# Candidate rows turned on TensorE instead of sent through DRAM, later column sums, and a new order in the last blocks and the first expert

## The chip, the cores and the metric

The kernel runs on one core of one Trainium2 chip. The metric is the time of one execution on the device, in microseconds (us). The engines are named as in the profile: PE is TensorE, DVE is VectorE, ACT is ScalarE, POOL is GpSimd, and SP is SyncE, which here only issues DMAs.

## The reference

One layer works on x of 2048 tokens by 1024 features (float32). `m` holds six modulation vectors made from the conditioning vector c.

```
h   = modulate(rms_norm(x), sh1, sc1)
b, c_, v = split(h @ w_in)                        # 1024 x 3072
x   = x + g1 * ((b * conv3(c_ * v)) @ w_out)      # short gated convolution
h2  = modulate(rms_norm(x), sh2, sc2)
aff = softmax(h2 @ w_router)                      # 16 experts
g, idx = top_k(aff.T, 256)                        # each expert picks its 256 best tokens
for each expert e:
    xs  = h2[idx[e]]
    hid = silu(xs @ w_gate[e]) * (xs @ w_up[e])
    x[idx[e]] += g2 * (g[e] * (hid @ w_down[e]))
```

So before an expert can work, the 256 greatest of 2048 values of its column of aff must be known, in which order does not matter beyond the pairing of g and idx.

## The kernel before, in words

A float32 product is done as three products of halves: high x high, low x high and high x low. The high half of a weight piece is a rounding copy by ACT (L247, tile `raw` to tile `ws`), the low half is what is left, a subtraction by DVE (L257). A piece is 128 by 2 by 512 elements, 512 KB. `raw` has five buffers in the expert stage. `split_high(n)` and `split_low(n)` emit the splits of all pieces up to n, and `split_to(n)` both.

The order of instructions on each engine is written out by hand: an engine works through its instructions in the order of the program's text, and only semaphores between engines delay it.

The stages, in this order: modulation, input product and convolution (to some 530 us); the output product by 16 blocks of 128 tokens, tb = 0 to 15; the choice of tokens; the experts.

The output product of a block takes eight steps k = 0 to 7 of TensorE (`out_mm`, L1196 to L1199, from pieces of the convolved input that DVE splits at L1094). Behind each step, `behind(tb, k)` emits some of the work on the block before: residual sum (`out_res`, DVE L1211, L1213, L1202), mean square (ACT L1214), norm (`out_h2`, DVE L1289, whose row goes to DRAM by POOL), the two 16-bit planes of the row (`halves_out`, ACT L1260), which SP stores and loads back transposed by a transposing DMA (L1265), joins (`router_join`, DVE L1274, ACT L1275 and L1277, DVE L1282), and the router's products (L1322, L1323, L1361), softmax (`router_sm`, to `aff` at DVE L1381). Blocks from 10 on are transposed by PE instead (`turn_xt`, `direct_mm`). SP also loads x's block (L1187) and the next convolved block (L1087).

For expert 0 the choice is made as the blocks go by. A candidate c is the column of 128 values of aff that block c gives. The values of the candidates so far are held as rows in the tile `ranked`, the same on all partitions. `rank_a(c)` compares all held values with candidate c's own (DVE L1439, with a count) and finds equal ones (POOL L1442, L1443). `rank_b(c)` sums the comparison's columns on PE into the PSUM tile `pr` (L1449), and `rank_c(c)` subtracts these sums from the counts (DVE L1454). `sort_a` to `sort_d` turn counts into a sorted list of 256 (one-hot comparisons L1460, products on PE, a copy on ACT, sums on POOL); this happens for candidates 0 to 7, then with 8 to 11, then with 12 to 14. A candidate's value column becomes a row in one of two ways. `row_store(c)` sends it to the DRAM tensor `values` by SP (L1416, 128 elements of 4 bytes), and `row_load(c)` reads it back to all partitions (L1421). `row_turn` transposes it on PE (L1428) and copies it with ACT (L1429). The table `steps`, made by `plan()`, says at which (block, step) each of these is emitted; the third number orders those of one step. Two PSUM buffers (pool `tp`) serve all of these small products.

After the last block follows a chain: the last sort, the gathers of expert 0's tokens (`fetch_first`, POOL), the router for block 15 (`last_row`, `router_sm`), the correction of the list by block 15's values, and the transposes of the gathered rows.

The experts come next. `gate_up(e, h)` makes half h of gate and up in eight steps (L1870, 24 products of 256 columns a step), and `down(e, dh)` a half of the down product in four (L1947 to L1949). Inside the steps, `between(k)` emits the choice for the other experts. For experts 1 and 2 it is `search_few`: in each round five thresholds are compared, some on DVE (L347), some on ACT (L351), the counts spread (DVE L354), summed on PE (L361, tile `pc`) and judged on DVE (L363 and on). For the other 13 it is `search_all`: a round has one threshold on DVE (L1690), two on ACT (L1694), a sum on PE (L1700) and the judgement on DVE (L1702 to L1708); `tick` emits one round. Gathering, transposing and joining of the next expert's tokens are `pick`, `turn` and `join`.

## Time and profile before

| | us |
|---|---|
| median of three runs | 1893.42 |
| the three runs | 1892.06, 1893.42, 1896.95 |
| the profiled execution | 1892.12 |
| its span, first to last instruction | 1890.3 |
| PE busy | 1815.3 |
| DVE busy | 1293.9 |
| ACT busy | 915.9 |
| POOL busy | 351.6 |

The mean granted clock of PE over the span was 0.983. Stages by the trace: blocks 6 to 10 of the residual work from 601 to 697 us, the last chain to 785.7, expert 0's gate and up to 841.3, expert 1's to 931.6. A table of windows gives, for each stretch, its length and then each engine's busy time with the count of its instructions, PE's granted clock, the share of the DMA engines and GB/s. A row of waits reads: engine, line that waited, what released it, us in total, times, the longest.

### The profile page before, as it was taken

The numbers are of one execution on the slowest core, as the hardware profiler recorded it, in microseconds if no ns is written. First come the engines' busy times: TensorE is split into PE (matmuls) and PEld (weight loads), VectorE is DVE, ScalarE is ACT, GpSimd is POOL, SyncE is SP. The second block draws the span as 40 slices with busy tenths as digits, with TensorE's granted clock in tenths as the row PEclk, the third lists the DMA queues.
The fourth block names the chain that finished last, engine by engine and source line by source line (L and its number), as shares of the span: only waits on it lengthen the run. The fifth ranks groups of instructions, "written<-read, shape, count | busy, mean of one in ns | idle before, by whom it ended". The sixth has DMA issues, their size and how long they took to land.

```text
span 1890.3 us, 29839 instructions
## 1 busy us (share of the span) xinstructions
PE 1815.3 (96%) x11542; PEld 1613.5 (85%) x11542; DVE 1293.9 (68%) x1924; ACT 915.9 (48%) x1263; POOL 351.6 (19%) x546
## 2 busy tenths in 40 slices
PE   7999999999999788897999999999999999999997
PEld 6888888888887666786999999999999999999996
DVE  6787778889766655686756666765666576566653
ACT  5565455334444443455544553544455355445542
POOL 2424101121012434301002102110210221021002
PEclk9999999999999889898999999999999999999999
DMA  9746665655689984566787879788887978888774
GB/s 340 239 168 205 197 211 178 157 160 174 162 262 235 183 155 153 167 202 167 217 239 246 227 224 264 219 245 243 253 228 224 260 223 242 246 250 230 224 229 83
DMA packets 316782, 403.25 MB, mean 213 GB/s; under 512 B 109652, under 2 KB 181248, under 8 KB 316640
## 3 DMA queue, kind: packets, MB, share of 16 engines
q1 hardware_dynamic: 291024, 310.08, 55.3%
q0 software_dynamic: 25616, 91.26, 17.5%
q8 instruction: 90, 1.47, 0.3%
q14 instruction: 52, 0.43, 0.1%
HBM read 316.86 MB, written 63.46 MB: 201 GB/s over the span
## 4 chain that ended last, share of the span: by engine, by line
PE 55%; DVE 4%; ACT 1%; issue 1%; POOL 1%; DMA 1%; POOLq 0%; ACTq 0%; DVEq 0%
PE pm L1870 36%; PE pm L1947 6%; PE pm L1949 6%; PE pm L1948 6%; DVE ws L257 1%; DMA ranked<-values 1%; ACT hit L1694 0%; DVE xt L1213 0%; DVE hit L347 0%; DVE u L1211 0%; PE pi L1803 0%; ACT ws L247 0%; DVE u L1202 0%; PE pm L1196 0%; DMA xs<-hscr,idx 0%
## 5 line engine op out<-in xcount | busy, mean ns | idle before, releaser
L1870 PE MATMUL pm<-xT,ws 128*128 128x256 f32 x6144 | 712.6, 278 | 0.5 <-DVE ws L257 0.5
L1870 PEld LDWEIGHTS pm<-xT,ws 128*128 128x128 f32 x6144 | 709.4, 189 | 3.2 <-DVE ws L257 0.9
L257 DVE TENSOR_TENSOR ws<-raw,ws 128x1024 fp32r<-128x1024 f32 x389 | 462.7, 1222 | 272.7 <-ACT ws L247 272.2
L247 ACT ACTIVATE ws<-raw 128x1024 fp32r<-128x1024 f32 x389 | 393.2, 1051 | 395.3 <-PE pm L1870 314.3
L1977 POOL DMA_INDIRECT out_dram<-ot,idx x30 | 100.6, 3354 | 600.0 <-DVE ot L1966 596.0
L1947 PE MATMUL pm<-ws,hT 128*128 128x512 f32 x504 | 201.1, 399 | 0.0
L1949 PE MATMUL pm<-ws,hT 128*128 128x512 f32 x504 | 200.4, 398 | 0.0
L1948 PE MATMUL pm<-ws,hT 128*128 128x512 f32 x504 | 199.2, 395 | 0.0
L899 PE MATMUL pm<-tg,sb 128*128 128x512 f32 x472 | 184.8, 391 | 0.8 <-ACT cx L966 0.8
L901 PE MATMUL pm<-tg,sb 128*128 128x512 f32 x472 | 183.8, 389 | 0.0
L900 PE MATMUL pm<-tg,sb 128*128 128x512 f32 x472 | 183.8, 389 | 0.0
L879 DVE TENSOR_TENSOR sb<-raw,sb 128x512 fp32r<-128x512 f32 x144 | 99.0, 690 | 59.3 <-ACT sb L878 58.0
L878 ACT ACTIVATE sb<-raw 128x512 fp32r<-128x512 f32 x144 | 88.7, 626 | 64.6 <-DVE raw L887 14.5
L1949 PEld LDWEIGHTS pm<-ws,hT 128*128 128x128 f32 x504 | 96.0, 191 | 20.6
L1948 PEld LDWEIGHTS pm<-ws,hT 128*128 128x128 f32 x504 | 96.1, 191 | 19.9
L1947 PEld LDWEIGHTS pm<-ws,hT 128*128 128x128 f32 x504 | 95.9, 190 | 19.1
L1196 PE MATMUL pm<-ws,hl 128*128 128x512 f32 x256 | 109.5, 428 | 0.1
L1811 POOL DMA_INDIRECT xs<-hhalf,idx x30 | 42.5, 1416 | 337.6 <-issue 212.8
L899 PEld LDWEIGHTS pm<-tg,sb 128*128 128x128 f32 x472 | 88.6, 188 | 19.5 <-ACT cx L966 1.2
L1197 PE MATMUL pm<-ws,hl 128*128 128x512 f32 x256 | 104.6, 408 | 0.0
L901 PEld LDWEIGHTS pm<-tg,sb 128*128 128x128 f32 x472 | 88.6, 188 | 18.5
L900 PEld LDWEIGHTS pm<-tg,sb 128*128 128x128 f32 x472 | 88.6, 188 | 18.0
(446 smaller groups left out, 2361.4 us busy)
## 6 DMA issues: line engine op xcount, KB each, us to landing
raw<-in_moe_w_gate_dram SPq DMA_DIRECT2D x128, 512.0 KB, 5.0
raw<-in_moe_w_up_dram SPq DMA_DIRECT2D x128, 512.0 KB, 4.1
raw<-in_moe_w_down_dram SPq DMA_DIRECT2D x128, 512.0 KB, 4.7
raw<-in_sc_w_in_dram SPq DMA_DIRECT2D x42, 512.0 KB, 4.6
aw<-in_ada_w_dram POOLq DMA_DIRECT2D x32, 512.0 KB, 5.1
xt<-in_x_dram SPq DMA_DIRECT2D x31, 512.0 KB, 6.6
fu<-fscr SPq DMA_DIRECT2D x23, 512.0 KB, 4.5
hl<-in_ada_w_dram SPq DMA_DIRECT2D x32, 256.0 KB, 6.6
```

What stands on the lines that cost most here:

```text
L247: nc.scalar.activation(t[:, 0], raws[n_high], AF.Copy)
L257: (eng or nc.vector).tensor_sub(t[:, 1, ..., s], raw[..., s], t[:, 0, ..., s].bitcast(F32))
L899: nc.tensor.matmul(o, t[:, 0, j], r[:, 0], start=(first and j == 0), stop=False, skip_group_check=True)
L900: nc.tensor.matmul(o, t[:, 1, j], r[:, 0], start=False, stop=False, skip_group_check=True)
L901: nc.tensor.matmul(o, t[:, 0, j], r[:, 1], start=False, stop=end, skip_group_check=True)
L1196: nc.tensor.matmul(ps[h], vh[:, k], w[:, 0, half(h)], start=(k == 0), stop=False)
L1197: nc.tensor.matmul(ps[h], vh[:, k], w[:, 1, half(h)], start=False, stop=False)
L1870: nc.tensor.matmul(o, w[:, i // 2, j, c0], xT[:, i % 2, k], start=(k == i == 0 and f % 2 == 0), stop=(k == KD - 1 and i == 2), skip_group_ ...
L1947: nc.tensor.matmul(ps[s], h, w[:, 0, j], start=(k == 0), stop=False)
L1948: nc.tensor.matmul(ps[s], h, w[:, 1, j], start=False, stop=False)
L1949: nc.tensor.matmul(ps[s], l, w[:, 0, j], start=False, stop=(k == KD - 1))
L1977: st = nc.gpsimd.indirect_dma_start(out=out_rows, out_offset=bass.IndirectOffsetOnAxis(ap=idx_of[e][:, s:s + 1], axis=0), in_=ots[s], in_o ...
```

## The change

1. `row_store`, `row_load` and the tensor `values` are gone. All candidates' rows are made by `row_turn`, the first four in one call with four transposes. The table `plan()` gives each candidate five places: the turn t, the comparison a, the sums b, the count d.
2. `rank_b` is three steps behind `rank_a` for candidates 0 to 7, four for 8, two for 9 to 12, and `rank_c` up to two steps behind `rank_b`. `sort_a` to `sort_d` for candidates 0 to 7 and 8 to 11 move accordingly.
3. In block 15 the norm of block 14, the two last comparisons, their sums and the last sort come at other steps. The two gathers of expert 0 are issued before `best` is summed (`sort_v`), the second one first. The planes of blocks 14 and 15 are copied by POOL instead of ACT.
4. In `search_few` two thresholds are on DVE and three on ACT (before: three and two), and the next base is computed by POOL. It begins one step later. In expert 0's products a piece's low half is split at the step that needs it, and high halves three pieces ahead; its terms are emitted in another order. In `down` the high half is split before the round instead of after it, for expert 0 one piece ahead. `search_all` is spread wider: five of the eight steps of expert 0's down product have a `tick` (before: all), eleven of expert 1's sixteen, and the rest is in expert 2's first products.

The diff, cut to its core:

```diff
-SPLITS = {0: (1, 3, 4, 5, 6, 7, 8, 9), 1: (11, 12, 13, 15, 16, 17, 19, 20)}
+SPLITS = {(0, 0): (0, 1, 2, 3, 4, 5, 6, 7), (0, 1): (9, 10, 11, 12, 13, 14, 15, 16), (1, 0): (28, 29, 30, 31, 32, 33, 34, 35),
+          (1, 1): (37, 38, 39, 40, 41, 43, 44, 45)}
+DOWN_SPLITS = {(0, 0): (18, 19, 20, 21), (0, 1): (23, 24, 25, 26)}
...
-                for j in (3, 4, 0, 1, 2):
+                for j in (2, 3, 4, 0, 1):
                     hit = scratch(j, n)
-                    if j < 3:
+                    if j < 2:
...
-                    nbase = small_tile("nbase", n=2)
-                    nc.vector.tensor_scalar(nbase, biasq[:, it + 1], neg, None, op0=ALU.add)
+                    nbase = small_tile("nbase", n=3)
+                    nc.gpsimd.tensor_scalar(nbase, biasq[:, it + 1], neg, None, op0=ALU.add)
...
-        def halves_out(tb, u, hs=slice(0, 2)):
+        def halves_out(tb, u, hs=slice(0, 2), eng=None):
...
-            nc.scalar.activation(uh[:, hs], u.bitcast(U16).rearrange("p (d h) -> p h d", h=2)[:, hs], AF.Copy)
+            planes = u.bitcast(U16).rearrange("p (d h) -> p h d", h=2)[:, hs]
+            if eng:
+                eng.tensor_copy(uh[:, hs], planes)
+            else:
+                nc.scalar.activation(uh[:, hs], planes, AF.Copy)
...
-        def row_store(c, n=1):
-            nc.sync.dma_start(bass.AP(tensor=values.tensor, offset=values.offset + c * P, ap=[[1, P], [P, n]]),
-                              value(c, n))
-
-        def row_load(c, n=1):
-            i = place(c)
-            nc.sync.dma_start(ranked[:, i * P:(i + n) * P],
-                              bass.AP(tensor=values.tensor, offset=values.offset + c * P, ap=[[0, P], [1, n * P]]))
...
-        def sort_c():
+        def sort_c(values=True):
             pk = small.tile([P, 2, 5], F32, name="pk", tag="pk", bufs=2)
             nc.scalar.activation(pk, pi_of[0], AF.Copy)
+            if values:
+                sort_v(pk)
+            return pk
+
+        def sort_v(pk):
             nc.gpsimd.tensor_add(best, pk[:, :, 2], pk[:, :, 3])
             nc.gpsimd.tensor_add(best, best, pk[:, :, 4])
-            return pk
         def sort_d(pk):
...
         def plan():
-            for c, b, k in ((4, 6, 5), (5, 7, 5), (6, 8, 5), (8, 10, 5), (10, 11, 1)):
-                steps[b, k, 8] = lambda c=c: row_store(c)
-                steps[b + (k == 5), 0 if k == 5 else 4, 8] = lambda c=c: row_load(c)
-            steps[5, 6, 8] = lambda: row_store(0, 4)
-            steps[6, 1, 8] = lambda: row_load(0, 4)
-            for c, a, b in ((0, (6, 4), (6, 7)), (1, (6, 7), (7, 3)), (2, (7, 4), (7, 7)), (3, (7, 7), (8, 3)),
-                            (4, (8, 4), (8, 7)), (5, (8, 7), (9, 3)), (6, (9, 4), (9, 7)), (7, (9, 7), (10, 3)),
-                            (8, (11, 4), (11, 6)), (9, (11, 7), (12, 2)), (10, (11, 7), (12, 3)),
-                            (11, (12, 5), (12, 7)), (12, (13, 6), (14, 1))):
-                steps[(*a, 4 + c % 2)] = lambda c=c: rank_a(c)
-                steps[(*b, 0)] = lambda c=c: rank_b(c)
-                steps[(*((b[0], 3) if c in (9, 10) else b), 1 + c % 2)] = lambda c=c: rank_c(c)
-            steps[9, 7, 3] = lambda: row_turn(7, value(7))
-            steps[11, 7, 3] = lambda: row_turn(3, value(9))
-            steps[12, 4, 3] = lambda: row_turn(5, value(11))
-            steps[13, 5, 4] = lambda: row_turn(2, value(12))
-            pk = []
-            for c, a, b, d in ((7, (10, 4), (10, 7), (11, 1)), (11, (12, 7), (13, 2), (13, 5))):
-                steps[(*a, 6)] = lambda c=c: sort_a(c)
+            for c, t, a, b, d in ((0, (5, 7), (6, 4), (6, 7), (7, 1)), (1, None, (6, 7), (7, 3), (7, 4)),
+                                  (2, None, (7, 4), (7, 7), (8, 1)), (3, None, (7, 7), (8, 3), (8, 4)),
+                                  (4, (6, 7), (8, 4), (8, 7), (9, 1)), (5, (7, 7), (8, 7), (9, 3), (9, 4)),
+                                  (6, (8, 7), (9, 4), (9, 7), (10, 1)), (7, (9, 7), (10, 4), (10, 7), (10, 7)),
+                                  (8, (10, 7), (11, 6), (12, 2), (12, 3)), (9, (11, 7), (12, 4), (12, 6), (12, 7)),
+                                  (10, (11, 5), (12, 5), (12, 7), (12, 7)), (11, (12, 5), (12, 6), (13, 0), (13, 0)),
+                                  (12, (13, 6), (13, 7), (14, 1), (14, 1))):
+                early = -4 if c == 11 else 0
+                if t:
+                    steps[(*t, 7)] = lambda c=c: row_turn(place(c), value(c, 1 if c else 4))
+                steps[(*a, 5)] = lambda c=c: rank_a(c)
+                steps[(*b, early + c % 2)] = lambda c=c: rank_b(c)
+                steps[(*d, early + 2 + c % 2)] = lambda c=c: rank_c(c)
+            for c, a, b, d in ((7, (10, 7), (11, 3), (11, 5)), (11, (13, 0), (13, 2), (13, 4))):
+                steps[(*a, -0.5 if c == 11 else 4)] = lambda c=c: sort_a(c)
                 steps[(*b, 6)] = lambda c=c: (sort_b(c), sort_d(sort_c()))
-                steps[(*d, 3)] = lambda: row_turn(0, best)
+                steps[(*d, 6)] = lambda: row_turn(0, best)
         plan()
         def behind(tb, k):
-            behind_block(tb, k)
-            for t in sorted(t for t in steps if t[:2] == (tb, k)):
-                steps.pop(t)()
+            for early in (True, False):
+                for t in sorted(t for t in steps if t[:2] == (tb, k) and (t[2] < 0) == early):
+                    steps.pop(t)()
+                if early:
+                    behind_block(tb, k)
...
                 router_sm(tb - 1, lambda: out_res(tb, 0, 0))
-                router_gate(tb - 1)
+                out_h2(tb - 1)
                 row_turn(3, value(tb - 2))
                 rank_a(tb - 2)
-                out_res(tb, 0, 1)
-                nc.vector.tensor_scalar(ss_of[tb][:, 2:3], ss_of[tb][:, 0:1], D * EPS, None, op0=ALU.add)
-            if k == 3:
+            if k == 2:
                 row_turn(4, value(tb - 1))
                 rank_a(tb - 1)
+                out_res(tb, 0, 1)
+                router_gate(tb - 1)
+                nc.vector.tensor_scalar(ss_of[tb][:, 2:3], ss_of[tb][:, 0:1], D * EPS, None, op0=ALU.add)
             if k == 4:
-                turn_xt(tb, 0)
                 rank_b(tb - 2)
                 rank_c(tb - 2)
-                out_h2(tb - 1)
                 split_high(first)
-            if k == 6:
+            if k == 5:
                 rank_b(tb - 1)
                 rank_c(tb - 1)
                 sort_a(tb - 1)
+            if k == 6:
+                turn_xt(tb, 0)
             if k == 7:
+                sort_b(tb - 1)
                 direct_mm(tb, 0)
-        sort_b(tb - 1)
-        pk_c = sort_c()
+        pk_c = sort_c(False)
...
+        fetch_first(1)
         fetch_first(0)
+        sort_v(pk_c)
         out_res_last(tb)
         out_rms(tb)
-        fetch_first(1)
         split_high(first + 1)
         out_scale(tb, 1)
         direct_mm(tb, 1)
         xt, u, r = xt_of[tb], u_of[tb], r_of_last[0]
         nc.sync.dma_start(out[0, L - P:L, :], xt)
+        halves_out(tb - 1, u_last[0], eng=nc.gpsimd)
...
-        halves_out(tb - 1, u_last[0])
...
-        nc.scalar.activation(uh[:, :, 0:QT], halves[:, :, 0:QT], AF.Copy)
-        nc.gpsimd.tensor_copy(uh[:, :, QT:D], halves[:, :, QT:D])
+        nc.gpsimd.tensor_copy(uh, halves)
...
-        late = 4 if (e, fh) == (0, 0) else 0
+        low = SPLITS.get((e, fh))
         for k in range(KD):
-            n = SPLITS[fh][k] + w_moe[0, 0, 0, 0] if e == 0 else w_moe[0, e, fh, k // 2] + n_split - 2 + k % 2
-            split_high(n)
+            n = w_moe[0, 0, 0, 0] + low[k] if low else w_moe[0, e, fh, k // 2] + n_split - 2 + k % 2
+            split_high(n + 3 * (e == 0))
             between(k)
             while n_done <= min(n, len(pieces) - 1):
                 split_low(n_done)
-            if k >= late:
+            if e:
                 products(k, (0, 1, 2))
-            elif k % 2:
+            elif (fh, k) == (0, 1):
                 for i in range(3):
+                    for kj in range(2):
+                        products(kj, (i,))
+            elif fh or k:
+                products(k, (0, 1))
+                if k % 2:
                     for kj in (k - 1, k):
-                        products(kj, (i,))
+                        products(kj, (2,))
...
+            low = DOWN_SPLITS.get((e, dh))
+            n = w_moe[0, 0, 0, 0] + low[kk] if low else w_moe[2, e, dh, kk] + n_split - 1
+            split_high(n + 1 if low else n)
             between(kk)
-            split_to(w_moe[2, e, dh, kk] + n_split - 1)
+            split_to(n)
...
-        if (k < 5 if h else k > 0):
+        if (k < 6 if h else k > 1):
             next(first_rounds, None)
-        if (h, k) == (1, 4):
+        if (h, k) == (1, 6):
             pick_oh(1)
-        if (h, k) == (1, 6):
+
+    def first_down(h, kk):
+        if (h, kk) == (0, 0):
             pick(1)
-        if (h, k) == (1, 7):
-            tick(k)
-
-    def first_down(h, kk):
-        tick(kk)
-        if h == 0 and kk < 2:
-            turn(1, kk)
-        if (h, kk) in ((0, 3), (1, 1)):
-            join(1, h)
+        elif (h, kk) not in ((1, 0), (1, 2)):
+            tick(kk)
+        if h == 0 and kk in (1, 2):
+            turn(1, kk - 1)
+        if (h, kk) in ((1, 0), (1, 2)):
+            join(1, kk // 2)
     def second_steps(h, k):
-        if h == 0 or k < 3:
+        if k in ((0, 2, 4, 6, 7), (0, 1, 2, 3, 5, 7))[h]:
             tick(k)
...
+    def third_steps(k):
+        if k < 4:
+            tick(k)
+        if k == 5:
+            for _ in rounds:
+                pass
+            pick_oh(3)
...
-            for _ in rounds:
-                pass
             continue
         else:
-            if e + 1 < E:
+            if 2 < e < E - 1:
                 pick_oh(e + 1)
-            gate_up(e, 0)
+            gate_up(e, 0, third_steps if e == 2 else lambda k: None)
```

Three places where instructions move. The first is SP's queue in blocks 7 and 8; rows are those that SP issues in order, and the DMA of `values` and `ranked` are the candidates' rows. Before:

```order
L1265 DMA_TRANSPOSE hl<-hl 128x16x128
L1087 DMA hl<-vscr 128x8x128
L1187 DMA xt<-in_x_dram 128x1024
L1421 DMA ranked<-values 128x128
L1416 DMA values<-aff 128x1
L1262 DMA hhalf<-hl 128x2048
```

After (line numbers shift with the diff: L1265 is now L1270, L1087 is L1088, L1187 is L1188, L1262 is L1267):

```order
L1270 DMA_TRANSPOSE hl<-hl 128x16x128
L1088 DMA hl<-vscr 128x8x128
L1188 DMA xt<-in_x_dram 128x1024
L1267 DMA hhalf<-hl 128x2048
L1270 DMA_TRANSPOSE hl<-hl 128x16x128
```

Nothing stands between the load of x and the next store of planes any more; twelve DMAs are gone from SP over the blocks.

The second is DVE in block 15, at the last two comparisons (L1439, now L1435), their counts (L1454, now L1450) and the norm of block 14 (L1289, now L1294). Before:

```order
L1439 SCALAR_TENSOR_TENSOR hits,count<-ranked,zero_1695,aff 128x512
L1213 TENSOR_TENSOR xt<-u,xt 128x512
L1202 TENSOR_TENSOR u<-xt,A2b 128x512
L1583 TENSOR_SCALAR ss<-ss 128x1
L1439 SCALAR_TENSOR_TENSOR hits,count<-ranked,zero_1695,aff 128x640
L1454 TENSOR_TENSOR count<-count,pr 128x4
L1289 SCALAR_TENSOR_TENSOR u<-u,rstd,sh2b 128x512 x2
L1454 TENSOR_TENSOR count<-count,pr 128x5
```

After:

```order
L1294 SCALAR_TENSOR_TENSOR u<-u,rstd,sh2b 128x512 x2
L1435 SCALAR_TENSOR_TENSOR hits,count<-ranked,zero_1694,aff 128x512
L1435 SCALAR_TENSOR_TENSOR hits,count<-ranked,zero_1694,aff 128x640
L1214 TENSOR_TENSOR xt<-u,xt 128x512
L1203 TENSOR_TENSOR u<-xt,A2b 128x512
L1585 TENSOR_SCALAR ss<-ss 128x1
L1450 TENSOR_TENSOR count<-count,pr 128x4
L1450 TENSOR_TENSOR count<-count,pr 128x5
```

The norm now comes ahead of both comparisons, and these stand together, ahead of the last residual sum.

The third is ACT in the down product of expert 0, with the comparisons of `search_all` (L1694, now L1693) and the high halves (L247, now L248). Before:

```order
L247 ACTIVATE ws<-raw 128x1024
L1694 ACTIVATE hit,cnt_1697<-keys,bias 128x256 x2
L247 ACTIVATE ws<-raw 128x1024
L1694 ACTIVATE hit,cnt_1698<-keys,nb_7757 128x256 x2
L247 ACTIVATE ws<-raw 128x1024
```

After:

```order
L1693 ACTIVATE hit,cnt_1696<-keys,nb_7771 128x256 x2
L248 ACTIVATE ws<-raw 128x1024 x2
L1693 ACTIVATE hit,cnt_1697<-keys,nb_7873 128x256 x2
L248 ACTIVATE ws<-raw 128x1024 x2
L1693 ACTIVATE hit,cnt_1696<-keys,bias 128x256 x2
```

Before, each high half stands behind a round's two comparisons; now two stand between rounds at several places, so that one is split ahead of the step that needs it.

More of the change, by code (lines that the diff above doesn't have):

```diff
@@ L65, in block_kernel @@
     rows = tc.dram_tile([4, D], F32, name="rows")
-    values = tc.dram_tile([L], F32, name="values")
     jp = consts.tile([P, P], I32, name="jp")
@@ L153, in constants @@
         nc.vector.tensor_scalar(mult, mult, repf, None, op0=ALU.add)
-        stepq = consts.tile([P, N_FEW[0] + N_FEW[1], 3], F32, name="stepq")
-        biasq = consts.tile([P, N_FEW[0] + N_FEW[1], 2], F32, name="biasq")
+        stepq = consts.tile([P, N_FEW[0] + N_FEW[1], 2], F32, name="stepq")
+        biasq = consts.tile([P, N_FEW[0] + N_FEW[1], 3], F32, name="biasq")
         for i in range(N_FEW[0] + N_FEW[1]):
@@ L350, in search_few @@
                         with nc.allow_low_precision(reason="integers up to 256"):
-                            nc.scalar.activation(hit, key, AF.Sign, bias=nb[:, j - 3:j - 2],
+                            nc.scalar.activation(hit, key, AF.Sign, bias=nb[:, j - 2:j - 1],
                                                  accum_out=cnt[:, j:j + 1])
@@ L365, in search_few @@
                 if not last:
-                    nb = small_tile("nb", n=2)
-                    nc.vector.scalar_tensor_tensor(nb, hd[:, 20:21].to_broadcast([P, 2]), -st, nbase, op0=ALU.mult,
+                    nb = small_tile("nb", n=3)
+                    nc.vector.scalar_tensor_tensor(nb, hd[:, 20:21].to_broadcast([P, 3]), -st, nbase, op0=ALU.mult,
                                                    op1=ALU.add)
@@ L1762, in search_first @@
         hit = [route.tile([P, CAP], BF, name="hit", tag="hit", bufs=3) for _ in range(2)]
-        thr = yield from search_few(lambda j, n: hit[j // 3][:, 0:n], keys)
+        thr = yield from search_few(lambda j, n: hit[j // 2 and 1][:, 0:n], keys)
         yield
```

8 lines of the change are left out of this document (4 added, 4 removed).

## The prediction

> **What bounds the kernel now.** I read the page's summary and its slices first, to see where TensorE is not full.
>
> ```profile
> PE 1815.3 (96%) x11542; PEld 1613.5 (85%) x11542; DVE 1293.9 (68%) x1924; ACT 915.9 (48%) x1263; POOL 351.6 (19%) x546
> PE   7999999999999788897999999999999999999997
> PEclk9999999999999889898999999999999999999999
> ```
>
> PE is busy for 96% and sits near full in all but slices 14 to 19, about 614 to 898 us (and the first). Those slices hold everything that the change touches. The table of windows splits them by stage (us, then busy time of each engine, granted clock, DMA share, GB/s):
>
> ```profile
> 601.00:697.30 96.30, 74.34 (x396) 58.26 (x395) 54.85 (x110) 36.81 (x59) 36.38 (x71) 0.86 0.87 167
> 697.30:760.00 62.70, 55.81 (x320) 45.50 (x319) 33.26 (x76) 22.62 (x49) 27.11 (x67) 0.95 0.55 154
> 760.00:785.70 25.70, 22.06 (x135) 18.19 (x134) 16.59 (x51) 11.76 (x25) 13.73 (x29) 0.87 0.50 162
> 785.70:840.00 54.30, 48.69 (x404) 47.50 (x404) 45.58 (x138) 28.37 (x53) 2.48 (x2) 0.94 0.59 187
> 840.00:894.00 54.00, 40.99 (x202) 33.36 (x200) 38.27 (x110) 31.80 (x69) 3.26 (x3) 0.87 0.70 186
> 894.00:954.40 60.40, 60.40 (x535) 60.31 (x532) 44.28 (x81) 33.68 (x47) 2.53 (x2) 1.00 0.77 226
> 954.40:1854.00 899.60, 899.60 (x6718) 842.64 (x6718) 578.54 (x656) 451.38 (x491) 132.20 (x65) 1.00 0.80 236
> 609.20:612.70 3.50, 3.50 (x10) 2.80 (x10) 1.23 (x1) 0.70 (x1) 0.71 (x2) 0.52 1.06 277
> ```
>
> From 894 us on PE never rests, so nothing is to be won there. Before that, PE's busy time times its granted clock is what a stage would take at full speed: 63.9 for blocks 6 to 10 (601 to 697.3), 53.0 for blocks 11 to 14, 19.2 for the last chain, 45.8 for the first expert's first products, 35.7 for its second ones. Stage less floor is 32.4, 9.7, 6.5, 8.5 and 18.3 us: 75.4 in all, the ceiling of any gain. The last row shows the second half of a stall's price: after a gap of 2.4 us (the longest of the last row of the next fence) the clock was 0.52 for 3.5 us, which loses 1.7 us more.
>
> What PE waits for, over the whole run:
>
> ```profile
> PE pc L1700 <- ACT hit L1694: 13.0, 6, 3.4
> PE pr L1449 <- DVE hits L1439: 9.9, 3, 6.4
> PE pr L1449 <- POOL equal L1443: 8.6, 5, 4.7
> PE pc L361 <- DVE each L354: 4.2, 2, 4.0
> PE pl L1361 <- ACT lt L1329: 3.4, 2, 2.4
> ```
>
> The second and third are the column sums of the ranking. DVE's own waits in 601 to 697.3 say what stands behind them:
>
> ```profile
> DVE hits L1439 <- DMA ranked<-values: 15.2, 3, 7.2
> DVE hl L1274 <- DMA hl<-hl: 5.2, 2, 2.9
> DVE xt L1213 <- DMA xt<-in_x_dram: 3.6, 1, 3.6
> DVE hits L1439 <- ACT ranked L1429: 0.7, 1, 0.7
> ```
>
> So PE waits for comparisons, and these wait for rows that go to DRAM and come back. DVE also waits for the transposing DMA and for x. SP's timeline (start, duration, instruction) shows what these have to do with the rows:
>
> ```profile
> 588.14 3.44 SPq L1265 DMA_TRANSPOSE hl<-hl  x1
> 596.20 0.37 SPq L1416 DMA_DIRECT2D values<-aff  x1
> 602.02 8.48 SPq L1265 DMA_TRANSPOSE hl<-hl  x1
> ...
> 681.51 4.84 SPq L1265 DMA_TRANSPOSE hl<-hl  x1
> ```
>
> The four transposes that follow a store of candidates within 6 us hold SP for 8.5 to 9.2 us; the one at 681.51, with no store ahead of it, holds it 4.84, like those before the first store. The loads of hl and xt are queued behind each. That is a correlation: four cases to six.
>
> **The change, part by part**, against the profiled run (1892.12 us, span 1890.3).
>
> *Rows by TensorE, blocks 6 to 10.* DVE's four waits sum to 24.7 us, and 96.3 - 24.7 = 71.6 is DVE's own chain, with what it waits for on ACT. 71.6 lies above PE's floor of 63.9, so DVE sets the pace, and the whole 24.7 counts only if transposes and xt come earlier too. If they do not, only the waits for rows go: 15.2 + 0.7 = 15.9. If DVE's lag is taken up by PE's slack, PE's floor gives 32.4. I take 24, near DVE's sum. What is added there is nine transposed columns more than before and their copies:
>
> ```profile
> L1428 PE MATMUL pt<-identf,aff x4: 273/288/473, 676.2 to 747.4; 128*128 128x128 f32 x4
> L1429 ACT ACTIVATE ranked<-pt x6: 257/271/386, 681.0 to 747.8; 128x128 f32<-128x128 f32 x4, 128x256 f32<-128x256 f32 x2
> ```
>
> Nine times 0.29 (weights load beside) is 2.6 us of PE, of which half falls into gaps that DVE's pace leaves: +1.5 (0 to 2.6). ACT has 36.81 busy of 96.3, which covers the copies.
>
> *Column sums later.* The rank sums of candidates 0 to 7 stay three steps behind (7, 4 to 7, 7 and so on); what moves is the count that follows, which holds its PSUM buffer one or two steps longer, and candidates 8 to 12. With *the other order of the last blocks* I cost this in 697.3 to 760 by the stage's gap of 9.7: DVE's waits for rows there are those of 560 to 910 us less those above,
>
> ```profile
> POOL equal L1442 <- DMA ranked<-values: 31.6, 5, 8.6
> DVE hits L1439 <- DMA ranked<-values: 24.7, 5, 7.2
> ```
>
> 24.7 - 15.2 = 9.5 us. I take -7 (0 to -9.7). In 760 to 785.7 the two gathers leave earlier (PE waited 1.5 for xs there) and sort_b no longer stands behind the slower engine: -2 (+2 to -6.5). POOL gets two copies of 2048 elements in place of ACT; its 13.7 busy of 25.7 covers them. Nothing reads them before expert 2.
>
> *Search of few in the first products.* Stage now 54.3. The wait for `each`, 4.2, falls to one comparison less on DVE. Against that, the high half is split three pieces ahead with five raw buffers, so a buffer comes free at a low split and its next piece must land, be split high behind the ACT comparisons, and be split low within two steps:
>
> ```profile
> L351 ACT ACTIVATE hit<-keys,nb 128x128 bf16<-128x128 f32 x10 | 4.0, 402 | 10.8 <-DVE nb L367 10.6
> L351 ACT ACTIVATION_READ_ACCUMULATOR hit<-keys,nb 128x1 f32 x10 | 1.9, 186 | 0.0
> DMA to landing us min/median/max: 3.6/4.4/8.5
> L257 DVE TENSOR_TENSOR ws<-raw,ws 128x1024 fp32r<-128x1024 f32 x389 | 462.7, 1222 | 272.7 <-ACT ws L247 272.2
> L247 ACT ACTIVATE ws<-raw 128x1024 fp32r<-128x1024 f32 x389 | 393.2, 1051 | 395.3 <-PE pm L1870 314.3
> L1870 PE MATMUL pm<-xT,ws 128*128 128x256 f32 x6144 | 712.6, 278 | 0.5 <-DVE ws L257 0.5
> ```
>
> (The landing is that of the tile raw from 775 to 850.) 4.4 + 1.05 + 3 comparisons of 0.59 + 1.22 + 0.2 for `each` is 8.6 us in two steps, where PE needs 2 x 24 products of 0.116 = 5.6. If all eight pairs ran so: 68.9, +14.6. If none did: the floor, -8.5. The first three pieces are split beforehand, and after the seventh round ACT is free; walking it through I get 30 us for the first half, as now, and 29 for the second against 25. I take +3.
>
> *Search for all, second products.* The chain of a round now, by the timeline:
>
> ```profile
> 850.37 0.16 DVE L1702 SCALAR_TENSOR_TENSOR hd<-pc,need 128x3 f32<-128x3 f32 x1
> 850.96 0.51 ACT L1694 ACTIVATE hit<-keys,nb 128x256 bf16<-128x256 f32 x1 [2.14 <-DVE nb L1708]
> 851.96 1.04 ACT L247 ACTIVATE ws<-raw 128x1024 fp32r<-128x1024 f32 x1
> 852.11 0.37 PE L1700 MATMUL pc<-cnt,same 128*128 128x4 f32 x1 [2.94 <-ACT hit L1694]
> 853.03 1.23 DVE L257 TENSOR_TENSOR ws<-raw,ws 128x1024 fp32r<-128x1024 f32 x1 [1.58 <-ACT ws L247]
> 854.18 0.15 DVE L1702 SCALAR_TENSOR_TENSOR hd<-pc,need 128x3 f32<-128x3 f32 x1
> ```
>
> Round to round is 3.8 us, and PE has 12 matmuls of 0.23 = 2.8 between. DVE idles 1.58 because the high split stands behind two comparisons on ACT. With the high half split one step earlier, DVE's path is 1.7 (850.37 to 852.11) + 0.4 + 1.22 = 3.3: the excess falls from 1.0 to 0.5 a round, and three of the eight steps of the down product have no round. Half of the 18.3 goes: -9 (0 to -18.3). The rounds that move to experts 1 and 2 lie beside a full PE (DVE 44.28 of 60.40, then 578.54 of 899.60): 0; if that cover failed, some four rounds at 1 us of DVE each (850.37 to the end of the comparison that follows) would cost 4.
>
> **Sum:** -24 + 1.5 - 7 - 2 + 3 - 9 = -37.5, so 1854.6; the median of the runs shown is 1.3 above the profiled run, within their spread, so I say 1855 for the median.
>
> The Trainium skill (TensorE: Matmul & The Clock Gate, Part 1: The HAM clock gate) says that the clock halves after about 3.4 us of idle window. The row 609.20:612.70 speaks against it as a threshold: there 2.41 us was enough. By the rule, the gaps of 1 to 2 us that I leave in the searches would cost no clock, and the sum would be about 3 us lower, near 1852.
>
> **The rivals.** (a) *PE takes up all the slack*: no gap long enough for the slow clock is left, and blocks and the search for all fall to their floors: -32.4 + 2.6 - 9.7 - 2 + 3 - 18.3 = -57, 1835. For it: clock and waits come and go together in the windows. Against: DVE's chain of 71.6. (b) *The transposes stay slow*, because the stores only happened to run beside the same traffic: blocks give 15.9 in place of 24: 1863. Against: 4.84 at 681.51; for: only four slow cases. (c) *The first expert gives nothing*: the searches pay in one place what they win in the other (+3 and 0, or +12 and -9): 1864. For: DVE is busy 45.58 of 54.3 there. (d) *A swap of waits*: PE stands at the transpose of a candidate until its value is ready, and each of five blocks pays a gap of 2.4 with 1.7 of clock, +20: 1875. Against: the transposes are put at step 7, and aff of the previous block is done by then in the timeline. (e) *Slower*: raw pieces of the first products land late. The price is 8 x (L + 4.2) - 54.3, by the loop above, for a landing of L; it eats the other terms' 40.5 at L = 7.7 and gives 1899 at 8.5, the longest of the row. Against: the median 4.4, and loads that ask for 187 GB/s there where 236 are moved later. (f) *The change does nothing* of what it says: the rows might not be what DVE waits for. The wait rows name them, so under 0.02: 1892.
>
> **How the numbers follow.** Forecast 0.44, its own range 1845 to 1864 (each term at half its way to a bound); (a) 0.14, (b) 0.17, (c) 0.13, (d) 0.06, (e) 0.04, (f) 0.02. The range 1833 to 1876 takes in (a) to (d) and leaves (e), (f) and the tails. 0.3%, 5.7 us, is about what a measurement of this kernel tells from no change. Faster by more: everything but (e) and (f), less a tail: 0.93; within: 0.04; slower: 0.03.
>
> **What would show it.** Right: no row of waits of DVE or POOL for ranked by DMA; transposes near 4 to 5 us all through the blocks; blocks 6 to 10 in about 72 us at a clock over 0.95; PE's wait for `hit` down to some 6 us; the first products at 57. Wrong: transposes still over 8 us (b); PE waiting at the candidates' transpose, or at a comparison that now waits for ACT's copy (d); PE waiting for ws or DVE for raw in the first products (e); a stretch after 954 us in which PE is no longer full.

## The result, and the profile after

The changed kernel takes 1876.38 us (median of four runs, 1873.94 to 1878.71), the kernel before 1892.74 (four runs, 1890.98 to 1896.95). The ratio is 0.991, with a 95% interval of 0.9889 to 0.9932. So it is faster by 16 us, where I forecast 38: the direction is right and the size is less than half. The profiled execution, the slowest of the four, took 1878.71 us with a span of 1876.9, 13.4 less than the span before.

The page of the changed kernel, slices of PE and of its granted clock:

```profile
PE 1809.7 (96%) x11551; PEld 1611.9 (86%) x11551; DVE 1292.1 (69%) x1905; ACT 918.7 (49%) x1281; POOL 356.2 (19%) x552
PE   7999999999999998788899999999999999999997
PEclk9999999999999998898999999999999999999999
```

The hollow that began at slice 14 now begins at slice 16, and it is no shallower there. The table of windows of the changed kernel, cut at its own stages (length, busy times, clock, DMA share, GB/s):

```profile
600.10:672.00 71.90, 67.16 (x395) 54.08 (x394) 54.78 (x109) 38.63 (x64) 37.56 (x71) 1.00 0.79 229
672.00:733.40 61.40, 55.90 (x331) 45.68 (x330) 33.93 (x78) 22.53 (x49) 26.92 (x66) 0.92 0.41 142
733.40:759.10 25.70, 21.49 (x130) 17.34 (x128) 17.41 (x50) 9.23 (x23) 15.57 (x31) 0.87 0.44 155
759.10:801.30 42.20, 31.79 (x206) 30.39 (x206) 19.41 (x66) 19.59 (x50) 1.63 (x4) 0.84 0.37 118
```

Blocks 6 to 10 run at full clock. Blocks 11 to 14 and the first half of expert 0's products do not. The waits of PE in the changed kernel name other things than before:

```profile
PE pm L1869 <- DVE ws L258: 9.0, 4, 2.6
PE pm L1952 <- DVE ws L258: 6.5, 2, 5.7
PE pc L1699 <- ACT hit L1693: 5.2, 3, 2.6
PE pc L362 <- DVE each L355: 5.0, 4, 3.5
PE pr L1445 <- DVE count L1450: 4.0, 3, 1.5
PE pt L1424 <- POOL best L1480: 3.4, 1, 3.4
PE pT L378 <- DVE tbits L326: 1.7, 1, 1.7
PE pcount L1732 <- DVE ge L1726: 1.5, 1, 1.5
```

(L1869 and L258 are the L1870 and L257 of before, L1952 the L1948, L1699 the L1700.) PE's waits for DVE's comparisons against rows (9.9 us before) are gone, and those for POOL's are down from 8.6 to 2.1 us; the long ones are now for low halves of weights.

By stage, in us, from the traces (a block's start is its first residual sum on DVE, a half of gate and up ends with its last Silu on ACT):

| stage | before | after | change | forecast |
|---|---|---|---|---|
| blocks 6 to 10 | 96.3 | 71.9 | -24.4 | -24 + 1.5 |
| blocks 11 to 14 | 63.3 | 61.4 | -1.9 | -7 |
| last chain | 25.1 | 25.7 | +0.6 | -2 |
| expert 0, first half | 30.5 | 42.2 | +11.7 | +3 with the next |
| expert 0, second half | 25.9 | 28.5 | +2.6 | |
| expert 0's down, expert 1's first half | 66.9 | 60.1 | -6.8 | -9 |
| expert 1's second, expert 2's first half | 45.9 | 51.5 | +5.6 | 0 |

They sum to -12.6, and 0.9 more was won before block 6. From there on both kernels run alike.

### The profile page after: what moved, and what is told of

Its sections match the earlier page's. It is cut to its first block, busy times and chain, and to the rows that moved or that the text cites. A ratio compares the mean times of both kernels' runs of the same rounds, so it can differ in the third digit from the quotient of the medians.

```text
span 1876.9 us, 29830 instructions
## 1 busy us (share of the span) xinstructions
PE 1809.7 (96%) x11551; PEld 1611.9 (86%) x11551; DVE 1292.1 (69%) x1905; ACT 918.7 (49%) x1281; POOL 356.2 (19%) x552
## 4 chain that ended last, share of the span: by engine, by line
PE 53%; DVE 1%; ACT 1%; DMA 1%; issue 0%; POOLq 0%; POOL 0%; ACTq 0%; DVEq 0%; SPq 0%
PE pm L1869 35%; PE pm L1951 6%; PE pm L1953 6%; PE pm L1952 6%; DMA tr<-xs 1%; DVE ws L258 1%; PE pi L1802 0%; ACT hit L1693 0%; ACT xT L1853 0%; ACT full L1850 0%; DVE xT L1854 0%; ACT ws L248 0%; DVE sg L1895 0%; DVE hT L1899 0%; ACT hT L1898 0%
## 5 line engine op out<-in xcount | busy, mean ns | idle before, releaser
L1869 PE MATMUL pm<-xT,ws 128*128 128x256 f32 x6144 | 719.9, 279 | 9.0 <-DVE ws L258 9.0
L1869 PEld LDWEIGHTS pm<-xT,ws 128*128 128x128 f32 x6144 | 715.6, 190 | 12.2 <-DVE ws L258 9.8
L258 DVE TENSOR_TENSOR ws<-raw,ws 128x1024 fp32r<-128x1024 f32 x389 | 463.3, 1222 | 261.9 <-ACT ws L248 261.9
L248 ACT ACTIVATE ws<-raw 128x1024 fp32r<-128x1024 f32 x389 | 393.7, 1051 | 418.8 <-PE pm L1869 305.6
L1952 PE MATMUL pm<-ws,hT 128*128 128x512 f32 x504 | 198.2, 393 | 6.5 <-DVE ws L258 6.5
L880 DVE TENSOR_TENSOR sb<-raw,sb 128x512 fp32r<-128x512 f32 x144 | 99.0, 690 | 59.1 <-ACT sb L879 57.8
L1952 PEld LDWEIGHTS pm<-ws,hT 128*128 128x128 f32 x504 | 95.2, 189 | 26.9 <-DVE ws L258 7.2
L1197 PE MATMUL pm<-ws,hl 128*128 128x512 f32 x256 | 106.1, 414 | 0.0
L1198 PE MATMUL pm<-ws,hl 128*128 128x512 f32 x256 | 101.5, 397 | 0.0
```

Of the source, the lines that this page charges most:

```text
L248: nc.scalar.activation(t[:, 0], raws[n_high], AF.Copy)
L258: (eng or nc.vector).tensor_sub(t[:, 1, ..., s], raw[..., s], t[:, 0, ..., s].bitcast(F32))
L1197: nc.tensor.matmul(ps[h], vh[:, k], w[:, 0, half(h)], start=(k == 0), stop=False)
L1198: nc.tensor.matmul(ps[h], vh[:, k], w[:, 1, half(h)], start=False, stop=False)
L1869: nc.tensor.matmul(o, w[:, i // 2, j, c0], xT[:, i % 2, k], start=(k == i == 0 and f % 2 == 0), stop=(k == KD - 1 and i == 2), skip_group_ ...
L1952: nc.tensor.matmul(ps[s], h, w[:, 1, j], start=False, stop=False)
```

## The experiments

Each run's difference is to the kernel before in the same comparison. Stages of single traces tell smaller effects than the times do, though a stage can also vary from one execution to the next.

### The two halves of the change, each alone

Parts 1 to 3 with the experts of before, and the experts' part alone on the kernel before. Of the diff shown above, the first has the hunks from `halves_out` to `uh`, the second the rest.

> The kernel before with parts 1 to 3 of the change alone (rows by TensorE, later sums, the other order of the last blocks); the experts' part is the one of before. By my reading of the two traces the blocks and the last chain save 26.6 us (26.6 earlier at the first product of expert 0) and the experts then take what they took before: 1893 - 26.6 = 1866. Rival: part of the 14 us that expert 0's products lost comes from starting them earlier after the faster blocks (loads not yet there), then the kernel stands above 1872 and the stretch from the first product to the end of the second half is over 60 us where it was 55.6.

Measured: 1867.0 (before 1889.1), ratio 0.9879 (0.986 to 0.9899). The first product starts at 758.6, and the two halves take 30.1 and 25.5 us, the stages after them 66.9 and 45.9, as before to 0.4 us. Starting earlier costs the experts nothing.

> The kernel before with part 4 alone (search of few, splits, spread of the search for all). If the stages are independent it loses what the traces show, 13 us: 1906, with the first product half near 41 us. Rival: the loss needs the faster blocks ahead of it, then 1885 to 1893.

Measured: 1900.0 (before 1889.1), ratio 1.0054 (1.0036 to 1.0072). So the change is a gain and a loss laid together, and part 4 alone makes the kernel slower, without the faster blocks. The loss is 11 us, where I expected 13. Its halves took 38.8 and 28.5 us.

### What slowed the transposing DMAs

The kernel of parts 1 to 3, with the six old stores put back on SP; nothing reads them:

```diff
+            for c, b, k in ((4, 6, 5), (5, 7, 5), (6, 8, 5), (8, 10, 5), (10, 11, 1)):
+                steps[b, k, 8] = lambda c=c: row_store(c)
+            steps[5, 6, 8] = lambda: row_store(0, 4)
```

> Rows by TensorE and the other parts 1 to 3 with the experts' part of before, plus the six old stores of candidates to DRAM at their old places in SP's order; nothing reads them. Theory (the stores of 128 elements of 4 bytes make the transposes behind them slow, and these make the join and x late): the four transposes that follow a store within 6 us take 8 us or more instead of 4.3 to 5.2, blocks 6 to 10 grow by 5.2 + 3.6 = 8.8 us, the kernel stands that much above the one without the stores (1867). Rival (the loads to all partitions, or the waits of SP for them, made them slow): transposes stay at 5, time within 3 us of 1867.

SP's timeline of the changed kernel, where no stores are:

```profile
613.66 5.20 SPq L1270 DMA_TRANSPOSE hl<-hl  x1
627.69 4.81 SPq L1270 DMA_TRANSPOSE hl<-hl  x1
641.86 4.91 SPq L1270 DMA_TRANSPOSE hl<-hl  x1
```

and of the kernel with the stores put back:

```profile
613.61 0.32 SPq L1420 DMA_DIRECT2D values<-aff  x1
618.96 6.62 SPq L1269 DMA_TRANSPOSE hl<-hl  x1
627.48 0.32 SPq L1420 DMA_DIRECT2D values<-aff  x1
632.83 8.01 SPq L1269 DMA_TRANSPOSE hl<-hl  x1
643.29 0.38 SPq L1420 DMA_DIRECT2D values<-aff  x1
648.95 10.88 SPq L1269 DMA_TRANSPOSE hl<-hl  x1
667.02 4.03 SPq L1269 DMA_TRANSPOSE hl<-hl  x1
```

The transposes behind a store hold SP long again (6.6 to 10.9 us, and 7.7 for one at 602.54 behind the store at 596.72; two of the four are below the 8 I expected), the one without a store ahead does not. Blocks 6 to 10 take 83.0 us where the same kernel without the stores took 71.8: +11.2 for 8.8 expected. The kernel takes 1875.5 us, ratio 0.9906 (0.9889 to 0.9924), some 5 us by the ratios and 8 by the medians more than without them (0.9879 and 1867.0; the two are from different comparisons). The stores alone do it, without a load and without a wait for one.

### The loop of expert 0's first half

DVE's and PE's timelines of the changed kernel over two steps of this half (start, duration, instruction, idle time ahead of it and what ended that):

```profile
775.14 1.22 DVE L258 TENSOR_TENSOR ws<-raw,ws 128x1024 fp32r<-128x1024 f32 x1
779.81 0.18 DVE L364 SCALAR_TENSOR_TENSOR hdq<-pc,needq 128x20 f32<-128x20 f32 x1 [3.46 <-PE pc L362]
781.95 0.18 DVE L355 TENSOR_TENSOR each<-cntq,rep 128x20 fp32r<-128x20 f32 x1 [0.76 <-ACT hit L352]
782.04 1.22 DVE L258 TENSOR_TENSOR ws<-raw,ws 128x1024 fp32r<-128x1024 f32 x1
783.18 0.17 DVE L364 SCALAR_TENSOR_TENSOR hdq<-pc,needq 128x20 f32<-128x20 f32 x1
785.31 0.18 DVE L355 TENSOR_TENSOR each<-cntq,rep 128x20 fp32r<-128x20 f32 x1 [0.76 <-ACT hit L352]
785.40 1.22 DVE L258 TENSOR_TENSOR ws<-raw,ws 128x1024 fp32r<-128x1024 f32 x1
```

```profile
776.41 3.35 PE L1869 MATMUL pm<-xT,ws 128*128 128x256 f32 x15 [2.12 <-DVE ws L258]
779.55 0.22 PE L362 MATMUL pc<-each,sameq 128*128 128x20 f32 x1
782.18 0.28 PE L362 MATMUL pc<-each,sameq 128*128 128x20 f32 x1 [0.25 <-DVE each L355]
786.68 0.59 PE L1869 MATMUL pm<-xT,ws 128*128 128x256 f32 x2 [2.17 <-DVE ws L258]
```

(The second view ends at 787 us, within the last group of products.) The two engines take turns. In every other step PE has 16 products with low halves, and all but the first stand behind the low half that DVE makes in that step (775.14); the next round's sum `pc` stands on PE behind them (779.55); DVE can judge only then, having idled 3.46; and the low half that the next such products need (785.40) stands on DVE behind that round, another low half and another round, while PE idles 2.17. From 775.14 to 785.40 it is 10.3 us for two steps. Loads of raw pieces are waited for in this loop too, by ACT at its high halves, but in the loop shown that wait is not what holds it up (ACT's timeline):

```profile
776.88 1.06 ACT L248 ACTIVATE ws<-raw 128x1024 fp32r<-128x1024 f32 x1 [1.87 <-DMA raw<-in_moe_w_up_dram]
780.37 0.40 ACT L352 ACTIVATE hit<-keys,nb 128x128 bf16<-128x128 f32 x1 [2.42 <-DVE nb L368]
```

After the late high half ACT stands another 2.42 us for DVE's next base, so the 1.87 us of waiting for the load delay no comparison, and no low half on DVE waits for a high half in this loop. (It happens once more, 2.00 us before a high half at 787.28, and ACT then stands 2.69 us for DVE.) The next two runs tell the loop of turns from the loop that I had priced.

```diff
-SPLITS = {(0, 0): (0, 1, 2, 3, 4, 5, 6, 7), ...
+SPLITS = {(0, 0): (1, 2, 3, 4, 5, 6, 7, 8), ...
-            split_high(n + 3 * (e == 0))
+            split_high(n + (3 - (fh == 0)) * (e == 0))
```

> The changed kernel with the low halves of expert 0's first product half split one step ahead of their use (pieces 1 to 8 at steps 0 to 7), high halves where they were. Theory of turns (the low half stands on DVE behind the search round of the very step that needs it, and the round's sum stands on PE behind a step's products, so DVE and PE work in turns, 10.3 us for two steps): the products of a step run beside the round, the half falls from 40.8 to 30 or 33, the kernel to 1866 to 1869. Theory of loads (a raw buffer comes free, its load lands, is split high and split low within two steps, 8.6 us or more): the loop is as long as it was, buffers come free one step earlier only at the start, under 3 us: 1874 to 1877.

Measured: 1865.7 (before 1889.1), ratio 0.987 (0.9851 to 0.9889). The half takes 27.6 us, less than in either kernel, and at full clock. The row of windows for it, and PE's timeline of this kernel:

```profile
760.20:787.80 27.60, 24.59 (x207) 24.00 (x207) 20.07 (x67) 19.05 (x49) 1.63 (x4) 1.00 0.54 176
```

```profile
775.97 0.28 PE L362 MATMUL pc<-each,sameq 128*128 128x20 f32 x1 [0.64 <-DVE each L355]
776.10 4.02 PE L1869 MATMUL pm<-xT,ws 128*128 128x256 f32 x32
```

The low halves stand at 772.47 and 779.20 there, 6.7 us for two steps, and PE no longer waits for them.

```diff
-            split_high(n + 3 * (e == 0))
+            split_high(n + (e == 0))
```

> The changed kernel with the high halves of expert 0's products split one piece ahead instead of three. Theory of turns: the low half still waits for the round of its step, no gain, 1874 to 1880 (later high halves can add a little). Theory of loads: the load has two more pieces' time, the half falls by 8 or more, 1868 or less.

Measured: 1871.9 (before 1889.1), ratio 0.99 (0.988 to 0.9921). The time lies below what turns alone had, and above what loads had; the half takes 34.6 us. The trace tells the parts. PE still waits for a low half every two steps, 9.7 us apart here (773.79 to 783.45), so the loop of turns stands (PE's timeline of this kernel, to 785 us, within the last group):

```profile
773.79 2.73 PE L1869 MATMUL pm<-xT,ws 128*128 128x256 f32 x15 [2.19 <-DVE ws L258]
783.45 1.76 PE L1869 MATMUL pm<-xT,ws 128*128 128x256 f32 x13 [2.05 <-DVE ws L258]
```

What went is a start. In the first 10 us of the changed kernel's half, ACT stood at two high halves whose loads were not there, with the list of expert 0 (`pk`) behind them, DVE behind that, and PE behind DVE:

```profile
DVE idx L1830 <- ACT pk L1828: 2.7, 1, 2.7
PE pm L1869 <- DVE ws L258: 2.6, 1, 2.6
ACT ws L248 <- DMA raw<-in_moe_w_gate_dram: 1.4, 1, 1.4
ACT ws L248 <- DMA raw<-in_moe_w_up_dram: 1.4, 1, 1.4
```

None of these four is in the trace with one piece ahead. So loads do matter once, at the start, for about 3 us by these waits. Another 3 us or so of the difference is the same loop at a higher granted clock, 0.95 over the half instead of 0.84; this run does not show whether that comes of the edit. The half also varies by execution: where its code is the same as the changed kernel's, traces have 42.2, 41.4, 38.8, 38.8, 38.5, 37.9 and 37.6 us, with a clock of 0.84 to 0.95. Only the 27.6, and with less certainty the 34.6, stand clear of that.

```diff
-                    if j < 2:
+                    if j < 3:
-                    nc.gpsimd.tensor_scalar(nbase, biasq[:, it + 1], neg, None, op0=ALU.add)
+                    nc.vector.tensor_scalar(nbase, biasq[:, it + 1], neg, None, op0=ALU.add)
```

> The changed kernel with three thresholds of the search for few on DVE and two on ACT, and the next base on DVE, as before; splits and order of the products stay changed. Theory of turns (low half behind the round): the half of expert 0's first product stays over 36, with some 0.3 us less a round since DVE no longer waits 0.76 for ACT's third comparison. Rival (the third comparison on ACT, ahead of the high halves, is what slows the loop): the half falls to 33 or less.

Measured: 1877.8 (before 1891.0), ratio 0.9929 (0.9914 to 0.9944); the half takes 36.9 us. Who compares what is not what slowed the loop. Whether it saves the 2 us expected of it can't be seen beside the spread above.

### The transpose of the second sorted list

My first guess at what slowed blocks 11 to 14 was the first sort, which comes half a block later than before:

```diff
-(7, (9, 7), (10, 4), (10, 7), (10, 7))
+(7, (9, 6), (9, 7), (10, 3), (10, 3))
-for c, a, b, d in ((7, (10, 7), (11, 3), (11, 5)),
+for c, a, b, d in ((7, (10, 4), (10, 7), (11, 1)),
```

> The changed kernel with the comparison of candidate 7 and the first sort at the places they had before (block 9 step 7, block 10 steps 4 and 7, block 11 step 1). Theory (blocks 11 to 14 saved 2 us instead of 7 because this work came half a block later, onto that of candidates 8 to 11, and its row's transpose makes TensorE wait 3.4): 672 to 733 shortens by 3 to 6 us. Rival (DVE's work in these blocks sets their pace wherever the sort stands): within 2 us, or the loss only moves to blocks 10 and 11.

Measured: 1878.3 (before 1892.4), ratio 0.9923 (0.9905 to 0.9941). Blocks 11 to 14 take 62.3 us, and the wait for POOL is still there, 3.4 us. That guess was wrong. The timelines of POOL, PE and DVE of the changed kernel show where the wait is, in block 13:

```profile
709.77 0.25 POOL L1395 CAST aux<-aff 128x16 bf16<-128x16 f32 x1
712.62 0.72 POOL L1390 COPY affq<-aff 128x8 f32<-128x8 f32 x1
713.30 0.18 POOL L1479 TENSOR_TENSOR best<-pk 128x2 f32<-128x2 f32 x1
```

```profile
713.81 0.69 PE L1424 MATMUL pt<-identf,best 128*128 128x128 f32 x2 [3.41 <-POOL best L1480]
714.73 0.63 PE L1198 MATMUL pm<-ws,hl 128*128 128x512 f32 x1
715.15 0.63 PE L1197 MATMUL pm<-ws,hl 128*128 128x512 f32 x1
```

The list `pk` of candidates 8 to 11 is on ACT at 709.59. Its sum `best` stands on POOL behind the router's gate for the block before (709.77 to 713.3). PE stands before the transpose of `best`, with the block's products behind it, and then runs them at 0.42 us each instead of 0.23, to about 722. The table of steps had moved this transpose from (13, 5) to (13, 4).

```diff
-(11, (13, 0), (13, 2), (13, 4))
+(11, (13, 0), (13, 2), (13, 6))
```

> The changed kernel with the transpose of the second sorted list (candidates 8 to 11) at block 13 step 6 instead of step 4, where before had step 5. Theory (TensorE reaches this transpose while the list's values stand on POOL behind the router's gate of block 12, waits 3.4 us, and then runs at half clock to 722): the wait is under 0.5, the stretch from the start of block 13's residual to that of block 14's falls from 18.8 to 12 or 14, the kernel gains 5 to 7. Rival (the chain of list, comparison and sums sets the pace of these blocks wherever TensorE stands): the stretch stays over 17.

Measured: 1870.9 (before 1891.0), ratio 0.9902 (0.9887 to 0.9918). The wait is gone, block 13 takes 11.4 us instead of 18.9, and blocks 11 to 14 take 54.0, 9.3 less than before the change: nearly the whole ceiling of 9.7. The other traces with that transpose at step 4 have 59.1 to 62.3 for these blocks, so this is clear of their spread. DVE's wait for ACT's copy of a row in block 13, 8.7 us in the changed kernel, is down to 1.6 with it. The kernel's time alone does not show the 5 to 7 us expected: its interval overlaps the changed kernel's. One row of windows of this kernel, with PE's clock at 1.00 where the changed kernel has 0.92:

```profile
672.00:734.00 62.00, 58.32 (x369) 47.62 (x365) 41.83 (x99) 25.69 (x56) 29.81 (x71) 1.00 0.47 160
```

### The last blocks

Block 15, the gathers and the copies of planes as before (the diff's hunks from `router_sm(tb - 1` to `uh` undone).

> The changed kernel with block 15 and what follows it (order of norm, comparisons, sort, gathers; planes copied by ACT) as before. My prediction gave this part -2 us, the two traces together show +0.6 from block 14's residual to the first expert product (35.5 before, 36.1 after). Theory (the part moves waits about and wins nothing): 35 to 37, kernel within 2 us. Rival (it wins what was predicted, hidden by another loss in the changed kernel): 38 or more.

Measured: 1875.8 (before 1891.0), ratio 0.9917 (0.9899 to 0.9934); from block 14's residual to the first product it is 37.3 us, where the changed kernel has 36.1 and the kernel before 35.5. The part wins nothing that can be told. In the changed kernel PE's wait for the gathered rows (1.5 us before) is gone, and one for the affinity of block 15 (L1633, 1.7) has come; with the part undone it is the other way round (1.8 and 0.2).

### The down product and the search for all

In the changed kernel the gather of expert 1 moved into the down product. DVE stands at the join for its transposes, and PE behind DVE (timelines of DVE and PE):

```profile
849.98 0.74 DVE L1849 COPY full<-tr 128x1024 uint16<-128x1024 uint16 x1 [5.90 <-DMA tr<-xs]
853.57 1.22 DVE L258 TENSOR_TENSOR ws<-raw,ws 128x1024 fp32r<-128x1024 f32 x1
```

```profile
854.84 0.80 PE L1952 MATMUL pm<-ws,hT 128*128 128x512 f32 x1 [5.70 <-DVE ws L258]
```

```diff
+        if (h, k) == (1, 7):
+            pick(1)
...
-        if h == 0 and kk in (1, 2):
-            turn(1, kk - 1)
+        if h == 0 and kk in (0, 1):
+            turn(1, kk)
```

> The changed kernel with the gather of expert 1 issued at the last step of expert 0's products instead of the first of its down product, and the two transposes one step earlier; the joins stay. Theory (TensorE's longest wait in the down product, 5.7 us for a low half, is DVE standing at the join for the late transposes): that wait is gone or under 2, the stretch of down and expert 1's first half falls from 60 to 52 to 55, the kernel by 5 to 8. Rival (the low half is late because of the round and its splits): stretch within 2 us of 60.

The longest wait for a low half in that stretch falls from 5.7 to 2.4 us and the stretch from 60.1 to 56.1 (52 to 55 expected), of which expert 0's second half gives 1.6 back. The kernel takes 1877.1 (before 1892.4), ratio 0.9915 (0.9892 to 0.9938): no gain that its time shows.

```diff
-        if k in ((0, 2, 4, 6, 7), (0, 1, 2, 3, 5, 7))[h]:
-            tick(k)
+        tick(k)
```

> The changed kernel with a step of the search for all in every step of expert 1's products, so that hardly any is left for expert 2's first half. Theory (the last steps of the search put small products on TensorE's queue that wait for DVE, 1.7 and 1.5 us, where TensorE had no gap before): expert 2's first half falls from 26.7 to 23 or 24, expert 1's second rises by 0 to 2, the kernel gains 1 to 4. Rival (expert 2's first half is slow because its weights' splits are late): it stays at 26 or 27.

Expert 2's first half falls from 26.7 to 21.6 us, expert 1's second takes 26.5 instead of 24.8: -3.4 together, and the two waits (`tbits`, `ge`) are gone from PE's list. The kernel's time, 1876.0 (before 1892.4), ratio 0.9917 (0.99 to 0.9934), does not show it.

### The corrections together

The three edits shown above for the second list's transpose, the gather and the search for all, and the low halves one step ahead in both halves of expert 0:

```diff
-SPLITS = {(0, 0): (0, 1, 2, 3, 4, 5, 6, 7), (0, 1): (9, 10, 11, 12, 13, 14, 15, 16), ...
+SPLITS = {(0, 0): (1, 2, 3, 4, 5, 6, 7, 8), (0, 1): (10, 11, 12, 13, 14, 15, 16, 17), ...
-            split_high(n + 3 * (e == 0))
+            split_high(n + 2 * (e == 0))
```

> The changed kernel with the four corrections together: low halves of expert 0's products one step ahead in both halves, gather of expert 1 a step earlier, a step of the search for all in every step of expert 1's products, transpose of the second sorted list at step 6. By the stages measured alone: expert 0's first half -13, down stretch -3, experts 1 and 2 -3, block 13 -6; 1876 - 25 = 1851, 1848 to 1860. If the corrections only move waits (each frees DVE time that another stall takes): 1860 to 1866, no better than the low halves alone.

Measured: 1853.6 us (median of five, 1852.1 to 1860.2; before 1891.0), ratio 0.9805 (0.9791 to 0.9818). It beats both kernels, the changed one by some 20 us. Blocks 11 to 14 take 54.0 us, expert 0's halves 29.6 and 29.2, the down stretch 60.1, the next two halves 48.9 (by the trace of the slowest execution, 1860.2). So the gain of the earlier gather did not stay (a wait of 4.3 us for a low half is still in the down product), and neither did the low halves ahead help expert 0's second half, which had 28.5; the other gains did stay.

## Why the prediction was wrong

**Rows by TensorE, blocks 6 to 10: right, by its own steps.** DVE's chain without its four waits was to be 71.6 us, and the stage takes 71.9; none of the four is left in the trace. The correlation of stores and slow transposes was a cause, as the run with the stores put back shows; rival (b) falls. PE did not take up the rest, and rival (a) falls too: 67.16 us of PE at full clock in 71.9.

**Column sums and the other order, -7: wrong by a wait that I had not placed.** I costed the stage by the waits that go and looked at none of the transposes that the table of steps moves. One of them, one step earlier, put PE before POOL: 3.4 us of wait and some 4 of half clock. The run with that transpose at step 6 gets 9.3 us; the mechanism named was right, and what took its place was missed. Rival (d) had the right kind of stall, PE at a transpose whose value is not ready, but at the candidates' transposes, where no such wait is in PE's list, and not at the sorted list's. Its other sign, DVE's comparison waiting for ACT's copy, came once (8.7 us, above).

**The last chain, -2: mis-sized.** It is +0.6, and undoing the part makes it no better.

**First products, +3: the step that failed most.** The stage lost 14.3 us in the trace. Walking it through I had 30 us for the first half and 29 for the second: the second takes 28.5, and the first 42.2 (37.6 to 42.2 in the seven traces). I had a bound of +14.6, but from another loop, of raw buffers, landings and high halves, so that it comes near the 14.3 is luck. Of rival (e) the sign came, PE waiting for low halves, and not the cause, late loads, except for the 3 us or so at the start. The real loop is made of DVE and PE, with ACT's comparisons inside the round. I had noted that the low half is split at the step that needs it, and did not put that beside the round ahead of it on DVE and the sum behind the products on PE. Written down as a cycle (16 products of 0.116 to 0.2 us, 0.26 from the sum to the judgement, two rounds of 2.2, two low halves of 1.2) it gives 8.9 to 10.3 us for two steps, against the 5.6 that PE needs.

**Search for all, -9: 6.8, mis-sized by 2.** The high half ahead did what was said (PE's waits for `hit` fell from 13.0 to 5.2), and a join waiting for late transposes took part of it.

**The cover for the rounds that move, 0: failed.** I gave 4 us as its price, and it cost 5.6. PE being full there is not a cover: a step's small products stand in PE's own order, and PE waits for their inputs like for any other. Moving them back to expert 1 wins 5.1 us in one half for 1.7 in the other. Rival (c), that the first expert gives nothing, came nearest for the experts: it allowed +12 and -9, measured are +14.3 and -6.8, and these 5.6 came on top.

With the corrections the kernel comes out near the forecast, 1853.6 beside 1855, though not by the same terms: by its trace blocks 6 to 10 and 11 to 14 give about 2 us each more than forecast (-24.3 and -9.3), and the last chain 1 less, the down stretch 2 less, and the two halves behind it cost 3 that I had put at nothing. The prediction summed what the parts could win and took too little for what they queue behind.

## What to carry to other kernels

Where an engine's order is fixed by the program, list for each moved instruction what stands ahead of it on its own engine and what its input's producer stands behind; a full engine hides the work of others, but not a small instruction in its own order that waits. When a split or copy is made just at the step that needs it, write the cycle through both engines and add it up, since two engines that each have slack can still take turns. A rule of thumb for a gain worked out from waits: it is a ceiling until the place of every moved instruction is checked against the time its input is ready.

## What the runs showed of the hardware

In these kernels a store of candidates (128 elements of 4 bytes each, the first of them 512 elements), issued by the same engine, makes the transposing DMA behind it hold SP for 6.6 to 10.9 us instead of 4.0 to 5.2, though nothing reads what it stores and though it was issued over 5 us before. Why it does so no run here shows.

Gaps of PE of about the same length do not cost the same. In expert 0's half, gaps of 2.05 to 2.2 us every two steps (and one of 2.6 at the head of the first) came with a granted clock of 0.84 over the half in one kernel and 0.95 in another (42.20 and 34.60 us, windows of the changed kernel, above, and of the one with high halves one piece ahead):

```profile
760.70:795.30 34.60, 26.29 (x202) 25.09 (x202) 19.04 (x66) 17.05 (x47) 1.63 (x4) 0.95 0.44 136
```

After the gap of 2.19 us there, 15 products took 2.73 us; after that of 2.05, the 13 in view took 1.76. So the length of a gap alone does not say what it costs. The Trainium skill (TensorE: Matmul & The Clock Gate, Part 1: The HAM clock gate) calls the activity window free-running. That would fit these rows, if what a gap costs depends on where in the window it falls, but no run here shows the window. Its 3.4 us of idle window is not a length below which a gap is free, as 2.12 us at the head of 3.35 us for 15 products shows.
